# A decoder trunk on one core: the first stage in written order on all engines, with fill products on TensorE

## The chip, the core and the metric

The kernel runs on one core of a Trainium2 chip. The metric is the device time of one execution in microseconds; smaller is better. The core's engines work side by side, each through its own list of instructions in order: TensorE (PE in the profile, its weight loads PEld) multiplies, VectorE (DVE) and ScalarE (ACT) work elementwise, GpSimd (POOL) helps them, and SyncE (SP) issues the transfers. An engine that waits for a semaphore holds up everything behind it in its list.

## The reference

One layer of a decoder: a normed and modulated input goes through three token mixers, then through an MLP. What matters here is the very start and the first projections. In short:

```python
cond = silu(c)
mod = cond @ w_ada + b_ada                  # sh1, sc1, gt1, sh2, sc2, gt2
h = rms_norm(x, g_norm1) * (1.0 + sc1) + sh1
z = h @ w_in                                # q, keys, values, gates, inputs of the mixers
merged = sig(ga) * gmlp(z) @ w_up_a + sig(gb) * mlstm(z) @ w_up_b + sig(gc) * nsa(z) @ w_up_c
x = x + gt1 * (merged @ w_out)
h = rms_norm(x, g_norm2) * (1.0 + sc2) + sh2
x = x + gt2 * (square(relu(h @ w_mlp1)) @ w_mlp2)
out = rms_norm(x, g_final)
```

x is 512 x 1024, all in float32.

## The kernel before

The features are kept on the 128 partitions: h is eight blocks j of 128 features by 512 tokens. To keep float32's precision on TensorE, every operand is split into a high part in a reduced format (hi) and the rest (lo), and a product is made of hi x hi, hi x lo and lo x hi. The copy to hi is ScalarE's, the subtraction for lo is VectorE's or GpSimd's. So each block of weights goes through `w_raw` (loaded), `w_hi` and `w_lo`, the last two with two buffers each.

The first stage does this. The transfers bring the vectors, x as four blocks of 128 tokens in two halves (`x_in`), then for each feature block j the two columns of the modulation weights (`ada_raw`, 2 x 512 KB) and the first weights (`w_early`, 128 x 768). The condition goes through a silu and is spread over the partitions: `dgc` times ones gives `cond_T`, copied to `condb`. For each block of tokens ScalarE and VectorE sum the squares (L179, L181), GpSimd takes the power that makes the reciprocal root `r` (L185), both engines scale (L186, L187), TensorE transposes (L191, eight products) and both copy the transpose to `xT` (L194).

Then come eight rounds, one per feature block. `early_mod(j)` loads, splits the weights (`chunk`, L109 and L110) and makes the modulation's two sums: for j = 0 and 4 (`ADA_PE`) on TensorE, 16 products with one column each (L225, two passes each in the trace), for the others on VectorE, two sums over 1024 columns (L216) against `condb`. `early_h(j)` makes scale and offset `ab` (L228, L230), h (ScalarE, L232), `h_hi` (ScalarE, L94) and `h_lo` (VectorE, L95). TensorE then makes 18 products of the round: six hi x hi (L245) and six pairs of lo x hi and hi x lo (L249, L250), into six banks called `early`.

Behind the rounds the banks are evacuated: `early` 0 to 3 are the queries of eight heads (`q`, ScalarE L323, VectorE L324), 4 and 5 the keys (`khh` ScalarE, `kll` VectorE, L331 to L334). Meanwhile TensorE makes `zt` 0 and 1 (L120, L121, then L284), which VectorE turns into windows (`win`, L362, eight steps, and `win_r`, L369), the products of the small weights (`sm`, L421 to L426, four banks: two come free with q, two with kll), the compression of the windows (`hid`, `kcmp`, `vcmp`) and then `ztok`.

What sets the order: nothing is placed by hand but TensorE's list within the first stage, which stands in `with tc.manual_schedule(engines={PE})`. Everything else is put in order by a scheduler that simulates the engines while the program is built. So the instructions of other engines within the stage, and all that follows, may move when the stage is written otherwise.

Of the kernel before, what the change touches and what calls it, by code (L numbers as in the profile page):

```python
# [36 lines left out]
ADA_PE = (0, 4)  # L37
# [23 lines left out]
def trunk_kernel(ctx: ExitStack, tc: tile.TileContext, x, vecs, rows, late_rows, ada1, w_ada,  # L61
# [68 lines left out]
    def tsl(tb):  # L130
        return slice(tb * P, (tb + 1) * P)
# [4 lines left out]
    xt = []  # L136
# [22 lines left out]
    dgc = temp(first, "dgc", "ada", 6, width=D)  # L159
# [13 lines left out]
    for tb in range(NT):  # L173
        ss1 = small.tile([P, 2], F32, name="ss1", bufs=4)
        for hf in range(2):
            xi = xt[tb][hf]
            junk = temp(first, "junk", "ht", 3)
# [4 lines left out]
        r1 = small.tile([P, 1], F32, name="r1", bufs=4)  # L182
# [15 lines left out]
    accs_, ws_early = {}, {}

    def early_mod(j):  # L200


        raws = []
        for q in range(2):
            raw = temp(first, "ada_raw", "ada", 6, width=D)
# [4 lines left out]
        ws_early[j] = chunk(w_early[j], 768)  # L210
        if j in ADA_PE:
            accs_[j] = [(raws[k // 4][:, (k % 4) * 256:(k % 4) * 256 + 256], cond[:, k:k + 1]) for k in range(KD)]
            return
        accs_[j] = small.tile([P, 2], F32, name="ada_s2")
        for q in range(2):
            V.scalar_tensor_tensor(raws[q], raws[q], 1.0, condb, op0=ALU.mult, op1=ALU.mult,  # L216
                                   accum_out=accs_[j][:, q:q + 1])

    def early_h(j):
# [11 lines left out]
        h, hi, lo = temp(first, "h_tmp", "ht", 3), page("h", "h_hi", F32R), page("h", "h_lo", F32R)  # L231
# [1136 lines left out]
```

## Time and profile before

| | |
|---|---|
| median of 3 runs | 976.35 us (974.14 to 977.8) |
| the profiled execution | 972.84 us, its span in the trace 971.0 us |
| TensorE busy | 934.9 us, 96% of the span |
| VectorE, ScalarE, GpSimd busy | 606.3, 406.9, 168.1 us |
| mean granted clock of TensorE | 0.979 |

All times below are counted in us from the start of the span. The granted clock is 1.00 at 2.4 GHz and 0.50 at 1.2 GHz. A row of a timeline gives start, duration, engine, line, operation, what is written and read, how often, and in brackets how long the engine had been idle ahead of it and what released it. The chain of waits is followed back from the last instruction of the program to what released each step.

### The profile page before, as it was taken

The page shows a single profiled execution, that of the slowest core. Times are in us where ns is not written, and L with a number is a line of the kernel's source. Part 1 is how long each engine was busy: PE and PEld are TensorE (multiplying, and loading weights), DVE is VectorE, ACT ScalarE, POOL GpSimd, SP SyncE. Part 2 cuts the span into 40 slices and gives each one's busy share as a digit, 9 for nine tenths or more (in the row PEclk, how much of TensorE's full clock was granted, in tenths as well). Part 3 has the DMA queues.
Part 4 walks back from the last instruction along what each step waited for, and adds up shares of the span by engine and source line. Part 5 has one row for each costly group of instructions (what it writes and reads, how often), then busy time and mean ns, then how long its engine had stood idle before and what let it go on. Part 6 is the DMA issues. An engine that isn't in the chain of part 4 may idle for free.

```text
span 971.0 us, 12508 instructions
## 1 busy us (share of the span) xinstructions
PE 934.9 (96%) x4718; PEld 787.2 (81%) x4718; DVE 606.3 (62%) x1167; ACT 406.9 (42%) x786; POOL 168.1 (17%) x118
## 2 busy tenths in 40 slices
PE   5999998998999999999999998999999999999997
PEld 4789987797876888888988887988888888888886
DVE  7648588777389656656688889766424254442435
ACT  5465465665463444444333344544321223432221
POOL 3044342332344123113300003000000000000001
PEclk8899999998999999999999999999999999999999
DMA  9633210110231223222478872363233323223222
GB/s 338 231 124 100 67 44 23 44 45 22 65 109 65 67 94 99 69 86 87 160 239 257 301 246 88 91 191 121 93 103 89 106 87 106 90 88 107 87 87 87
DMA packets 34268, 111.71 MB, mean 115 GB/s; under 512 B 3936, under 2 KB 4128, under 8 KB 34208
## 3 DMA queue, kind: packets, MB, share of 16 engines
q1 hardware_dynamic: 34208, 110.91, 34.7%
q8 instruction: 37, 0.61, 0.3%
q14 instruction: 23, 0.19, 0.1%
HBM read 108.80 MB, written 2.10 MB: 114 GB/s over the span
## 4 chain that ended last, share of the span: by engine, by line
PE 84%; DVE 11%; ACT 2%; issue 1%; DMA 1%; SPq 0%; POOL 0%; POOLq 0%; ACTq 0%
PE tok L1096 7%; PE tok L1095 7%; PE tok L1097 7%; PE m L116 6%; PE m L115 6%; PE m L114 6%; PE zt L120 5%; PE zt L121 5%; PE zt L284 5%; PE ztok L896 5%; PE pv L557 2%; PE up L120 2%; PE up L121 2%; PE up L849 2%; PE pT L532 2%; PE zt L880 2%
## 5 line engine op out<-in xcount | busy, mean ns | idle before, releaser
L109 ACT CAST w_hi<-w_raw 128x1024 fp32r<-128x1024 f32 (+2 forms) x137 | 141.6, 1033 | 255.8 <-PE tok L1096 97.4
L110 DVE TENSOR_TENSOR w_lo<-w_raw,w_hi 128x1024 fp32r<-128x1024 f32 (+1 forms) x92 | 115.1, 1252 | 175.9 <-ACT w_hi L109 169.7
L110 POOL TENSOR_TENSOR w_lo<-w_raw,w_hi 128x1024 fp32r<-128x1024 f32 (+2 forms) x45 | 110.3, 2452 | 246.8 <-ACT w_hi L109 137.6
L120 PE MATMUL zt<-h_hi,w_hi 128*128 128x512 f32 x272 | 107.8, 396 | 0.0
L121 PE MATMUL zt<-h_lo,w_hi 128*128 128x512 f32 x272 | 107.3, 395 | 0.0
L116 PE MATMUL m<-h_hi,w_lo 128*128 128x512 f32 (+1 forms) x272 | 103.9, 382 | 0.0
L114 PE MATMUL m<-h_hi,w_hi 128*128 128x512 f32 (+1 forms) x272 | 103.8, 382 | 0.0
L115 PE MATMUL m<-h_lo,w_hi 128*128 128x512 f32 (+1 forms) x272 | 103.6, 381 | 0.0
L1096 PE MATMUL tok<-w_hi,f_lo 128*128 128x512 f32 (+1 forms) x232 | 88.6, 382 | 0.0
L1095 PE MATMUL tok<-w_hi,f_hi 128*128 128x512 f32 (+1 forms) x232 | 88.6, 382 | 0.0
L1097 PE MATMUL tok<-w_lo,f_hi 128*128 128x512 f32 (+1 forms) x232 | 84.3, 382 | 0.0
L284 PE MATMUL zt<-h_hi,w_lo 128*128 128x512 f32 x272 | 70.0, 393 | 0.0
L120 PEld LDWEIGHTS zt<-h_hi,w_hi 128*128 128x128 f32 x272 | 51.4, 189 | 10.9 <-ACT num_lo L778 0.4
L115 PEld LDWEIGHTS m<-h_lo,w_hi 128*128 128x128 f32 x272 | 51.1, 188 | 11.0
L121 PEld LDWEIGHTS zt<-h_lo,w_hi 128*128 128x128 f32 x272 | 51.5, 189 | 10.4
L114 PEld LDWEIGHTS m<-h_hi,w_hi 128*128 128x128 f32 x272 | 51.2, 188 | 10.5
L116 PEld LDWEIGHTS m<-h_hi,w_lo 128*128 128x128 f32 x272 | 51.1, 188 | 10.5
L284 PEld LDWEIGHTS zt<-h_hi,w_lo 128*128 128x128 f32 x272 | 50.8, 188 | 10.5
L1237 POOL TENSOR_TENSOR o_g<-x,gfin 128x512 f32<-128x512 f32 x1 | 1.3, 1293 | 310.9 <-DVE x L1141 310.9
L1095 PEld LDWEIGHTS tok<-w_hi,f_hi 128*128 128x128 f32 x232 | 43.6, 188 | 8.5
L1097 PEld LDWEIGHTS tok<-w_lo,f_hi 128*128 128x128 f32 x232 | 43.6, 188 | 8.5
L1096 PEld LDWEIGHTS tok<-w_hi,f_lo 128*128 128x128 f32 x232 | 43.6, 188 | 8.4
(388 smaller groups left out, 2000.9 us busy)
## 6 DMA issues: line engine op xcount, KB each, us to landing
w_raw<-in_w_m SPq DMA_DIRECT2D x64, 512.0 KB, 3.5
w_raw<-in_w_zt SPq DMA_DIRECT2D x38, 512.0 KB, 3.4
ada_raw<-in_w_ada SPq DMA_DIRECT2D x24, 512.0 KB, 4.9
ada_raw<-in_ada SPq DMA_DIRECT2D x14, 512.0 KB, 7.0
w_raw<-in_w_tok SPq DMA_DIRECT2D x12, 512.0 KB, 3.4
w_raw<-in_w_up SPq DMA_DIRECT2D x12, 512.0 KB, 3.5
w_raw<-in_w_out SPq DMA_DIRECT2D x8, 512.0 KB, 4.8
w_raw<-in_w_ada SPq DMA_DIRECT2D x8, 512.0 KB, 3.9
```

The lines of the kernel that those rows point to most:

```text
L109: V.tensor_copy(hi, raw) if dve_hi else A.copy(hi, raw)
L110: (G if pool_lo else V).tensor_tensor(lo, raw, f(hi), op=ALU.subtract)
L114: T.matmul(ps, ah, bh, start=first, stop=False)
L115: T.matmul(ps, ah, bl, start=False, stop=False)
L116: T.matmul(ps, al, bh, start=False, stop=last)
L120: T.matmul(ps, ah, bh, start=first, stop=False)
L121: T.matmul(ps, ah, bl, start=False, stop=False)
L284: T.matmul(ps, wl[:, tsl(k)], hh[k], start=False, stop=k == KD - 1)
L896: T.matmul(o, a_[k][:, tsl(tb)], w_[:, kk * 256:(kk + 1) * 256], start=k == 0 and tb % 2 == 0 and a_ is hh and w_ is wh, stop=k == KD - 1 ...
L1095: T.matmul(p_, ah_, wh, start=k == 0, stop=False)
L1096: T.matmul(p_, al_, wh, start=False, stop=False)
L1097: T.matmul(p_, ah_, wl, start=False, stop=k == 2 * n - 1)
```

## The change

It rewrites the first stage and leaves the arithmetic as it is.

- The stage stands in a manual order for TensorE, ScalarE, VectorE and GpSimd, not for TensorE alone: on these engines the order is that of the code. The transfers' order is still the scheduler's.
- The work on x is cut into four functions (`x_rms`, `x_scale`, `x_turn`, `x_copy`), called for different blocks of tokens in turn, so that the copy of a transpose comes a block after its scaling.
- `idle(n)` puts n products of ones by ones, 128 x 128, into a bank that nothing reads: 9, 4, 5, 3, 2 and 6 of them.
- Loads are written two rounds ahead (`early_load`), with seven buffers for `ada_raw` instead of six; the sums (`early_sums`), scale and offset (`early_mod`) and h with the split of the weights (`early_h`) are called for round j + 1 between the two halves of round j's products.
- Scratch for the squares and for h comes from other pages (tag "mr").

```diff
-    for hf in range(2):
-        cp = bank("T", "cond_T")
-        T.matmul(cp, ones, dgc[:, hf * 512:(hf + 1) * 512], start=True, stop=True)
-        A.copy(condb[:, hf * 512:(hf + 1) * 512], cp)
...
+    def idle(n):
+
+        for _ in range(n):
+            T.matmul(warm[:, 0:P], ones, ones, start=True, stop=True)
...
     def early_h(j):
-        tp = accs_.pop(j)
...
+
+        wh = stream.tile([P, D], F32R, name="w_hi", tag="hi")[:, :768]
+        wl = stream.tile([P, D], F32R, name="w_lo", tag="lo")[:, :768]
+        A.copy(wh, raw_early[j])
+        ab = abs_[j]
+        h, hi, lo = page("mr", "h_tmp"), page("h", "h_hi", F32R), page("h", "h_lo", F32R)
         A.activation(h, xT[j // 4][:, j % 4, :], AF.Identity, scale=ab[:, 0:1], bias=ab[:, 1:2])
         split(hi, lo, h)
+        V.tensor_tensor(wl, raw_early[j], f(wh), op=ALU.subtract)
+        ws_early[j] = wh, wl
...
-    with tc.manual_schedule(engines={mybir.EngineType.PE}):
+    raw_early, abs_, sums_ = {}, {}, {}
+    E_ = mybir.EngineType
+    with tc.manual_schedule(engines={E_.PE, E_.Activation, E_.DVE, E_.Pool}):
+        early_load(0)
+        early_load(1)
+        warm = bank("acc", "warm")
+        idle(9)
+        cps = [bank("T", "cond_T") for _ in range(2)]
+        for hf in range(2):
+            T.matmul(cps[hf], ones, dgc[:, hf * 512:(hf + 1) * 512], start=True, stop=True)
+        idle(4)
+        x_rms(0)
+        x_rms(1)
+        x_scale(0)
+        A.copy(condb[:, 0:512], cps[0])
+        x_turn(0)
+        idle(5)
+        x_rms(2)
+        x_scale(1)
+        x_copy(0)
+        x_turn(1)
+        idle(3)
+        x_rms(3)
+        x_scale(2)
+        x_copy(1)
+        A.copy(condb[:, 512:D], cps[1])
+        x_turn(2)
+        idle(2)
+        x_scale(3)
+        x_copy(2)
+        x_turn(3)
+        x_copy(3)
+        early_sums(0)
         early_mod(0)
+        idle(6)
         early_h(0)
+        early = [bank(t, "early") for t in ("mm", "mm", "S", "S", "acc", "acc")]
         for j in range(KD):
-            wh, wl = ws_early.pop(j)
-            if j + 1 < KD:
-                early_mod(j + 1)
+            wh, wl = ws_early[j]
+            if j + 2 < KD:
+                early_load(j + 2)
             for i in range(6):
                 T.matmul(early[i], wh[:, tsl(i)], hh[j], start=j == 0, stop=False)
             if j + 1 < KD:
+                if j + 1 not in sums_:
+                    early_sums(j + 1)
+                if j + 1 in ADA_PE and j + 2 < KD:
+                    early_sums(j + 2)
+                early_mod(j + 1)
                 early_h(j + 1)
             for i in range(6):
                 T.matmul(early[i], wh[:, tsl(i)], hl[j], start=False, stop=False)
                 T.matmul(early[i], wl[:, tsl(i)], hh[j], start=False, stop=j == KD - 1)
```

How the lists of the engines differ is shown at three places. The first is VectorE from the last copies of transposes on. The list before, in which `ada_s` are the sums of a round, `ab` its scale and offset, and `w_lo` the split of the weights:

```order
L194 COPY xT_128<-x_T 128x4x128
L110 TENSOR_TENSOR w_lo<-w_raw,w_hi 128x768
L216 SCALAR_TENSOR_TENSOR ada_raw,ada_s_318<-ada_raw,condb 128x1024 x2
L228 TENSOR_SCALAR ab<-ada_T,bsc_120,vec 128x1
L230 TENSOR_SCALAR ab<-ada_T,vec 128x1
L228 TENSOR_SCALAR ab<-ada_s_278,bsc_120,vec 128x1
L230 TENSOR_SCALAR ab<-ada_s_278,vec 128x1
L216 SCALAR_TENSOR_TENSOR ada_raw,ada_s_358<-ada_raw,condb 128x1024
L228 TENSOR_SCALAR ab<-ada_s_318,bsc_120,vec 128x1
L230 TENSOR_SCALAR ab<-ada_s_318,vec 128x1
L230 TENSOR_SCALAR ab<-ada_s_358,vec 128x1
L95 TENSOR_TENSOR h_lo<-h_tmp,h_hi 128x512
```

Before, the sums of rounds 1 to 3 (`ada_s_278`, `_318`, `_358`) stand ahead of the first `h_lo` or right behind it. The list of the changed kernel at the same place:

```order
L201 COPY xT_122<-x_T 128x4x128 x2
L242 TENSOR_SCALAR ab<-ada_T,bsc_120,vec 128x1
L244 TENSOR_SCALAR ab<-ada_T,vec 128x1
L95 TENSOR_TENSOR h_lo<-h_tmp,h_hi 128x512
L255 TENSOR_TENSOR w_lo<-w_raw,w_hi 128x768
L235 SCALAR_TENSOR_TENSOR ada_raw,ada_s_316<-ada_raw,condb 128x1024 x2
L242 TENSOR_SCALAR ab<-ada_s_316,bsc_120,vec 128x1
L244 TENSOR_SCALAR ab<-ada_s_316,vec 128x1
L95 TENSOR_TENSOR h_lo<-h_tmp,h_hi 128x512
L255 TENSOR_TENSOR w_lo<-w_raw,w_hi 128x768
L235 SCALAR_TENSOR_TENSOR ada_raw,ada_s_356<-ada_raw,condb 128x1024 x2
```

Now each round stands by itself: sums, `ab`, `h_lo`, `w_lo`, and only then the sums of the next round.

The second place is ScalarE at the end of the rounds. There `w_hi` of 768 columns is a round's, `w_hi` of 1024 columns is that of `zt`, and `q` the evacuation of the queries. Before:

```order
L109 CAST w_hi<-w_raw 128x1024
L368 CAST phi_r<-w_raw 128x16x64
L323 ACTIVATE q_0_604<-early 64x512
L323 ACTIVATE q_1_605<-early 64x512
L323 ACTIVATE q_2_606<-early 64x512
L109 CAST w_hi<-w_raw 128x1024
L323 ACTIVATE q_3_607<-early 64x512
L323 ACTIVATE q_4_612<-early 64x512
```

The evacuation of q 0 to 2 stands ahead of the weights of zt(1), the second `w_hi` of 1024 columns. In the changed kernel:

```order
L250 CAST w_hi<-w_raw 128x768
L109 CAST w_hi<-w_raw 128x1024
L253 ACTIVATE h_tmp<-xT_123,ab 128x512
L94 CAST h_hi<-h_tmp 128x512
L109 CAST w_hi<-w_raw 128x1024
L385 ACTIVATE q_0_634<-early 64x512
L430 CAST phi_r<-w_raw 128x16x64 x2
L385 ACTIVATE q_1_635<-early 64x512
L385 ACTIVATE q_2_636<-early 64x512
L385 ACTIVATE q_3_637<-early 64x512
L385 ACTIVATE q_4_642<-early 64x512
L109 CAST w_hi<-w_raw 128x864
```

The weights of zt(0) have moved ahead of the last round's h (and on TensorE fourteen of zt(0)'s products ahead of the last round's), and the weights of zt(1) and both phi stand ahead of or between the first q.

The third place is VectorE behind the rounds, where `win` is a window's step, `win_r` its split, and `kll` the evacuation of a key bank. In the changed kernel:

```order
L386 SCALAR_TENSOR_TENSOR q_0_634<-early,q_0_634 64x512
L386 SCALAR_TENSOR_TENSOR q_1_635<-early,q_1_635 64x512
L424 TENSOR_TENSOR win<-zt,vec 64x8x31 x5
L386 SCALAR_TENSOR_TENSOR q_2_636<-early,q_2_636 64x512
L424 TENSOR_TENSOR win<-zt,vec 64x8x31 x3
L386 SCALAR_TENSOR_TENSOR q_3_637<-early,q_3_637 64x512
L386 SCALAR_TENSOR_TENSOR q_4_642<-early,q_4_642 64x512
L424 TENSOR_TENSOR win<-zt,vec 64x8x31 x8
L431 TENSOR_TENSOR win_r<-win,win_r 128x16x64
L386 SCALAR_TENSOR_TENSOR q_5_643<-early,q_5_643 64x512
L386 SCALAR_TENSOR_TENSOR q_6_644<-early,q_6_644 64x512
L431 TENSOR_TENSOR win_r<-win,win_r 128x16x64
```

Before, seven q stood in a row ahead of the first window, and the first two kll ahead of and among the steps of the second; now both windows stand among the q, and all kll behind them.

## Rows read from the trace of the kernel before

**Rows 1.** Timeline of TensorE in stage one: start, us, operation, idle before.
```profile
5.04 3.78 PE L169 MATMUL cond_T<-dgc,ones 128*128 128x512 f32 x4 [5.04 <-DVE dgc L161]
...
13.88 1.71 PE L225 MATMUL ada_T<-cond,ada_raw 128*128 128x1 f32 x8
15.45 4.65 PE L191 MATMUL x_T<-ident,x_in 128*128 128x128 f32 x24
19.93 1.84 PE L225 MATMUL ada_T<-cond,ada_raw 128*128 128x1 f32 x16
26.52 2.93 PE L245 MATMUL early<-h_hi,w_hi 128*128 128x512 f32 x6 [4.74 <-ACT h_hi L94]
```

**Rows 2.** Timeline of VectorE in stage one.
```profile
13.88 0.48 DVE L187 TENSOR_SCALAR x_in<-x_in,r 128x512 f32<-128x512 f32 x1
...
21.71 1.22 DVE L216 SCALAR_TENSOR_TENSOR ada_raw<-ada_raw,condb 128x1024 f32<-128x1024 f32 x1
...
24.00 0.27 DVE L228 TENSOR_SCALAR ab<-ada_T,bsc,vec 128x1 f32<-128x1 f32 x1
```

**Rows 3.** The chain of waits up to 112 us: start, us, what.
```profile
32.27 1.36 PE early L245 x6
...
76.20 1.22 DVE win_r L369
...
86.14 0.71 DVE kll L333
```

**Rows 4.** Timeline of TensorE from round 3 to vcmp.
```profile
41.62 3.63 PE L225 MATMUL ada_T<-cond,ada_raw 128*128 128x1 f32 x32
45.11 0.48 PE L249 MATMUL early<-h_lo,w_hi 128*128 128x512 f32 x1
...
49.14 1.91 PE L245 MATMUL early<-h_hi,w_hi 128*128 128x512 f32 x6
...
69.47 1.98 PE L284 MATMUL zt<-h_hi,w_lo 128*128 128x512 f32 x8
...
94.99 0.33 PE L896 MATMUL ztok<-w_hi,h_hi 128*128 128x256 f32 x1
...
103.60 0.66 PE L399 MATMUL vcmp<-p,c_rep 64*128 64x64 f32 x4 [1.33 <-DVE c_rep L397]
```

**Rows 5.** Timeline of VectorE in round 3, whose h it waits for.
```profile
31.27 0.69 DVE L95 TENSOR_TENSOR h_lo<-h_tmp,h_hi 128x512 fp32r<-128x512 f32 x1 [1.54 <-ACT h_hi L94]
...
33.02 0.95 DVE L110 TENSOR_TENSOR w_lo<-w_raw,w_hi 128x768 fp32r<-128x768 f32 x1
```

**Rows 6.** Stretches: us, busy of PE, PEld, DVE, ACT, POOL, granted clock, DMA share, GB/s.
```profile
9.00:12.00 3.00, 0.63 (x6) 0.66 (x6) 2.46 (x10) 2.28 (x7) 1.42 (x3) 1.00 1.00 345
...
15.40:19.00 3.60, 3.60 (x18) 3.60 (x19) 3.21 (x5) 0.63 (x2) 0.00 (x0) 0.50 1.03 418
19.30:21.80 2.50, 2.48 (x24) 2.39 (x22) 2.50 (x5) 1.64 (x3) 0.00 (x0) 1.00 1.04 380
...
46.60:49.60 3.00, 3.00 (x9) 2.35 (x8) 3.00 (x10) 2.49 (x4) 0.22 (x2) 0.50 0.00 0
...
104.80:107.40 2.60, 2.60 (x14) 2.60 (x14) 0.00 (x0) 0.00 (x0) 1.40 (x1) 0.50 0.07 13
```

**Rows 7.** Timeline of ScalarE behind the rounds.
```profile
63.99 0.59 ACT L323 ACTIVATE q<-early 64x512 fp32r<-64x512 f32 x1
...
71.05 0.92 ACT L109 CAST w_hi<-w_raw 128x864 fp32r<-128x864 f32 x1
```

**Rows 8.** Timeline of VectorE behind the rounds.
```profile
71.84 3.00 DVE L362 TENSOR_TENSOR win<-zt,vec 64x248 f32<-64x248 f32 x8
...
95.18 1.95 DVE L95 TENSOR_TENSOR v<-v,v 128x256 fp32r<-128x256 f32 x1
...
98.35 0.49 DVE L95 TENSOR_TENSOR v<-v,v 128x256 fp32r<-128x256 f32 x1
```

**Rows 9.** Timeline of GpSimd at the same time.
```profile
94.45 2.40 POOL L110 TENSOR_TENSOR w_lo<-w_raw,w_hi 128x1024 fp32r<-128x1024 f32 x1 [1.60 <-ACT v L94]
```

More of the change, by code (lines that the diff above doesn't have):

```diff
@@ L157, in trunk_kernel @@
     V.tensor_scalar(cond, cth, 0.5, None, op0=ALU.mult)
-    dgc = temp(first, "dgc", "ada", 6, width=D)
+    dgc = temp(first, "dgc", "ada", 7, width=D)
     for k in range(KD):
@@ L164, in trunk_kernel, with x_rms @@
     V.tensor_scalar(bsc1, vec[:, V_SC1:V_SC1 + 8], 1.0, None, op0=ALU.add)
-    for hf in range(2):
-        cp = bank("T", "cond_T")
-        T.matmul(cp, ones, dgc[:, hf * 512:(hf + 1) * 512], start=True, stop=True)
-        A.copy(condb[:, hf * 512:(hf + 1) * 512], cp)
     xT = [first.tile([P, 4, S], F32, name=f"xT{hf}") for hf in range(2)]
-    for tb in range(NT):
+    r1s = {}
+    def x_rms(tb):
         ss1 = small.tile([P, 2], F32, name="ss1", bufs=4)
@@ L176, in trunk_kernel @@
             xi = xt[tb][hf]
-            junk = temp(first, "junk", "ht", 3)
+            junk = page("mr", "junk")
             if hf == 0:
@@ L181, in trunk_kernel @@
                 V.scalar_tensor_tensor(junk, xi, 1.0, xi, op0=ALU.mult, op1=ALU.mult, accum_out=ss1[:, 1:2])
-        r1 = small.tile([P, 1], F32, name="r1", bufs=4)
+        r1 = r1s[tb] = small.tile([P, 1], F32, name="r1", bufs=4)
         V.tensor_tensor(r1, ss1[:, 0:1], ss1[:, 1:2], op=ALU.add)
@@ L185, in trunk_kernel, with x_scale, x_turn, x_copy @@
         G.tensor_tensor(r1, r1, mhalf[:, 0:1], op=ALU.pow)
-        A.activation(xt[tb][0], xt[tb][0], AF.Copy, scale=r1)
-        V.tensor_scalar(xt[tb][1], xt[tb][1], r1, None, op0=ALU.mult)
+    def x_scale(tb):
+        A.activation(xt[tb][0], xt[tb][0], AF.Copy, scale=r1s[tb])
+        V.tensor_scalar(xt[tb][1], xt[tb][1], r1s[tb], None, op0=ALU.mult)
+    x_ps = {}
+    def x_turn(tb):
+        x_ps[tb] = [bank(("mm", "S", "acc")[(2 * tb + hf) % 3], "x_T") for hf in range(2)]
         for hf in range(2):
-            tp = bank(("mm", "S", "acc")[(2 * tb + hf) % 3], "x_T")
             for q in range(4):
-                T.transpose(tp[:, tsl(q)], xt[tb][hf][:, tsl(q)], ident)
+                T.transpose(x_ps[tb][hf][:, tsl(q)], xt[tb][hf][:, tsl(q)], ident)
+    def x_copy(tb):
+        for hf in range(2):
             dst = xT[hf][:, :, tsl(tb)]
-            src = tp.rearrange("p (q t) -> p q t", q=4)
+            src = x_ps[tb][hf].rearrange("p (q t) -> p q t", q=4)
             A.copy(dst, src) if hf else V.tensor_copy(dst, src)
+    def idle(n):
+        for _ in range(n):
+            T.matmul(warm[:, 0:P], ones, ones, start=True, stop=True)
     hh, hl = [], []
-    early = [bank(t, "early") for t in ("mm", "mm", "S", "S", "acc", "acc")]
     accs_, ws_early = {}, {}
-    def early_mod(j):
+    def early_load(j):
         raws = []
         for q in range(2):
-            raw = temp(first, "ada_raw", "ada", 6, width=D)
+            raw = temp(first, "ada_raw", "ada", 7, width=D)
             for c0 in range(0, D, 512 if j == 0 else D):
@@ L209, in early_mod, with early_sums @@
             raws.append(raw)
-        ws_early[j] = chunk(w_early[j], 768)
+        accs_[j] = raws
+        raw_early[j] = load(w_early[j], 768)
+    def early_sums(j):
+        raws = accs_[j]
         if j in ADA_PE:
[L212 to L219, printed above, removed]
-        tp = accs_.pop(j)
-        if j in ADA_PE:
-            ts_, tp = tp, bank("T", "ada_T")
-            for i, (a, c_) in enumerate(ts_):
-                for u in range(2):
-                    T.matmul(tp[:, u:u + 1], a[:, u * P:(u + 1) * P], c_, start=i == 0 and u == 0,
-                             stop=i == len(ts_) - 1 and u == 1)
-        ab = small.tile([P, 2], F32, name="ab")
+            tp = bank("T", "ada_T")
+            for k in range(KD):
+                for u in range(2):
+                    T.matmul(tp[:, u:u + 1], raws[k // 4][:, (k % 4) * 256 + u * P:(k % 4) * 256 + (u + 1) * P],
+                             cond[:, k:k + 1], start=k == 0 and u == 0, stop=k == KD - 1 and u == 1)
+        else:
+            tp = small.tile([P, 2], F32, name="ada_s2")
+            for q in range(2):
+                V.scalar_tensor_tensor(raws[q], raws[q], 1.0, condb, op0=ALU.mult, op1=ALU.mult,
+                                       accum_out=tp[:, q:q + 1])
+        sums_[j] = tp
+    def early_mod(j):
+        tp = sums_[j]
+        ab = abs_[j] = small.tile([P, 2], F32, name="ab")
         V.tensor_scalar(ab[:, 0:1], tp[:, 1:2], bsc1[:, j:j + 1], vec[:, V_G1 + j:V_G1 + j + 1], op0=ALU.add,
@@ L230, in early_h @@
         V.tensor_scalar(ab[:, 1:2], tp[:, 0:1], vec[:, V_SH1 + j:V_SH1 + j + 1], None, op0=ALU.add)
-        h, hi, lo = temp(first, "h_tmp", "ht", 3), page("h", "h_hi", F32R), page("h", "h_lo", F32R)
+    def early_h(j):
+        wh = stream.tile([P, D], F32R, name="w_hi", tag="hi")[:, :768]
[3 more added lines that the diff above has]
+        h, hi, lo = page("mr", "h_tmp"), page("h", "h_hi", F32R), page("h", "h_lo", F32R)
         A.activation(h, xT[j // 4][:, j % 4, :], AF.Identity, scale=ab[:, 0:1], bias=ab[:, 1:2])
         split(hi, lo, h)
+        V.tensor_tensor(wl, raw_early[j], f(wh), op=ALU.subtract)
+        ws_early[j] = wh, wl
         hh.append(hi)
         hl.append(lo)
-    with tc.manual_schedule(engines={mybir.EngineType.PE}):
+    raw_early, abs_, sums_ = {}, {}, {}
[6 more added lines that the diff above has]
+        cps = [bank("T", "cond_T") for _ in range(2)]
+        for hf in range(2):
+            T.matmul(cps[hf], ones, dgc[:, hf * 512:(hf + 1) * 512], start=True, stop=True)
[22 more added lines that the diff above has]
+        early_sums(0)
         early_mod(0)
+        idle(6)
         early_h(0)
+        early = [bank(t, "early") for t in ("mm", "mm", "S", "S", "acc", "acc")]
         for j in range(KD):
-            wh, wl = ws_early.pop(j)
-            if j + 1 < KD:
-                early_mod(j + 1)
+            wh, wl = ws_early[j]
+            if j + 2 < KD:
+                early_load(j + 2)
             for i in range(6):
```

## The prediction

> **What bounds the kernel now.** I read the page first, then TensorE's timeline from the start, the stretches with the granted clock, VectorE's timeline beside it, and last the chain of waits up to 112 us. TensorE is busy for 96% of the span, so a change of its work elsewhere would count in full; but the instruction order of all engines is the same again from about 112 us on, so only the first 112 us can differ, and what is won or lost there is carried to the end. In that stretch three things are to be seen. First, TensorE starts its real work late: the first product of block 0 starts at 26.52 [rows 1]. The products for the modulation of block 0 had ended at 19.93 + 1.84 = 21.77 [rows 1], but VectorE took their result only at 24.00, behind two sums for block 2 that stand ahead of it, the first at 21.71 [rows 2]. Second, up to about 58 us TensorE is the bound: 18 products of a block at 1.36 / 6 = 0.227 each, 4.09 in all [rows 3]. Third, from 64 to 87 us the chain runs through VectorE and ScalarE (the evacuation of q, the windows, k) and ends with a kll on VectorE at 86.14 [rows 3]; TensorE's products just keep up with them. So VectorE is the second bound here, and a change that hands it work later is paid for.
>
> I measure against a mark M: TensorE has done all products of the eight blocks and the first sixteen of zt(0). Before, M is 69.47 [rows 4].
>
> **Stage one: fills and order.** VectorE scales the last block of x at 13.88 + 0.48 = 14.4 even before [rows 2]; now one copy of a transpose stands ahead of that, so 14.4 to 15.0. The eight transposes behind it take 24 per 4.65, so 1.5, at the half clock [rows 1], and I bound them below by half of that: done at 15.2 to 16.5. Now the 16 modulation products of block 0 (32 passes in the trace) follow at once: 3.6 at the full clock [rows 4], or 4 x 1.71 = 6.8 at half [rows 1]. Then ab, about 0.4, and the 1.54 from the last ab to the end of h_hi [rows 5], with nothing ahead of them on VectorE any more. So h_hi(0) is ready between 20.7 and 25.2 instead of 26.5. I take 22.7, nearer to the full clock, since the fills keep TensorE at work from the start on: a gain of **3.8** (1.3 to 5.8).
>
> A fill, ones by ones 128x128, isn't in the trace. The nearest row is cond_T, four passes of 512 columns in 3.78 [rows 1], so by columns 2 x 0.24 = 0.47 at half clock; below it is bounded by two modulation passes, 0.22. The first nine, 4.2, thus all but fit into the 5.04 that TensorE waited for cond_T's operand; cond_T's result is first read by the sums of block 1, so what they run over is hidden. The fills between the transposes lie in waits for the scaled x. The last six cost 1.3 to 2.8 beside the 1.95 of ab and h; that can hold up block 0's products by 0.9, but not the chain of VectorE below, which starts at h_hi(0). If the cover is gone, it is 0.9.
>
> Where the clock stands at the modulation products decides most of that range. TensorE ran transposes alone from 15.45 to 19.9, and its granted clock went from 0.50 to 1.00 by 19.30 [rows 1, 6]: transposes were enough to raise it to 2.4 GHz from 1.2. The Trainium skill (TensorE: Matmul & The Clock Gate, Part 4: PE-mode transpose) says that the full clock does not engage for transposes as it does for matmuls; this trace does not agree. By the page the slow end, 25.2, would be the likelier one and the sum below 2.5 us higher.
>
> **The eight blocks.** This is where the gain goes. Before, VectorE made the sums of blocks 1 to 3 ahead, while TensorE still waited for block 0. Now its order is strict: h_lo(j), w_lo(j), two sums of j+1, ab(j+1), then a wait for ScalarE's h and h_hi, then h_lo(j+1). One round is 0.69 + 0.95 [rows 5] + 2.29 for the two sums (21.71 to 24.00, [rows 2]) + 0.4 + 1.54 [rows 5], less 0.1 where neighbours overlap: 5.8, against 4.09 for TensorE's block. So TensorE waits some 1.7 in each of the first three rounds, and block 3 starts 17.4 after h_hi(0). Block 3 holds the modulation products of block 4, 3.5 (41.62 to 45.11 [rows 4]), so it takes 7.6; block 4's round brings VectorE the sums of block 5 in that time. Blocks 4 and 5 are then TensorE's, 4.09 each; block 6 starts at +16.0, when its h_hi is ready, and ends at +20.1. Now zt(0) stands ahead of block 7 on TensorE; its weights' copy waits for block 6's buffer, so TensorE waits 1.0, then does 34 products, 7.7: M at +28.8. If the clock falls behind the modulation products as before (12 products in 49.14 - 45.11 = 4.03 for 2.72 [rows 4], clock 0.50 [rows 6]), +30.3. So 46.2 to 47.7 from h_hi(0) to M, where it was 69.47 - 26.5 = 43.0: a loss of 3.2 to 4.7, I take **3.8**. The half clock that the waits may bring in the first three rounds costs no more, since it only fills the waits.
>
> **From M to ztok.** Before, 94.99 - 69.47 = 25.5 [rows 4]. There VectorE began with q before M, since ScalarE evacuated q0 at 63.99 [rows 7]. Now ScalarE copies the weights of zt(1) first, which waits for block 7's buffer, so q0 starts at M + 1.0, then come both phi copies, and VectorE's q1 follows at M + 4.2. From there by the new orders: window 0 and q2, q3, q4 to 9.9 (eight windows take 3.00 [rows 8], a q 0.65), window 1 to 12.9, win_r 1.22 [rows 3] to 14.1, two q, win_r, q, two kll and the small steps between them to 19.9. The copy of the small weights, 0.92 [rows 7], stands behind q4 on ScalarE and ends at M + 9.6, though zt(1) is done at 7.3: a wait of 2.3. The third bank of sm waits for the second kll until 19.9, where TensorE is ready at 17.3: another 2.6. The rest is 10.1 of products. So ztok starts at M + 30.0: a loss of 4.5. If VectorE's chain runs without gaps it is 2.1 shorter, loss 2.4; if the second wait brings the half clock, 1.5 longer, loss 6.0. I take **5.0**.
>
> **vcmp.** Before, TensorE waited 1.33 ahead of it [rows 4] and then ran at 0.50 [rows 6], some 1.5 more. Now c_hid(1) no longer stands behind a table load, but vcmp comes only 32 products (3.8) behind ztok's start, with VectorE's copies of v in front of it. Between all of it gone, -2.8, and a wait 1.7 longer, I take **0**.
>
> **The DMA order** is nearly unchanged: seven buffers for ada instead of six let one more load go early. No round waits for a load, since each is issued a round or more ahead. The buffers of raw weights come free with w_lo, later than before, still in time.
>
> **Sum:** -3.8 + 3.8 + 5.0 + 0 = +5.0. The profiled execution took 972.84 (span 971.0), 3.5 below the median of the runs, 976.35; so 977.8 against that execution, and 981.4 as a median. The ends of the terms give -3.0 and +11.1, so 973.4 to 987.5.
>
> **Rivals.**
> (a) The stage comes out even or better, not slower: the fills hold 2.4 GHz through stage one (h_hi(0) at 20.7, -5.8), the blocks cost 3.2, VectorE's chain behind M has few gaps (+3.5) and half of vcmp's loss goes (-1.4): -0.5, 975.9. For it speaks that cond_T's four passes were followed by the full clock, 1.00 from 9 to 12 us [rows 6]; against it, that all ends must be met at once. It decides from h_hi(0) before 21.5 together with less than 4 us lost behind M.
> (b) VectorE and GpSimd get in each other's way. A v step of VectorE took 1.95 at 95.18, where the same took 0.49 at 98.35 [rows 8], while GpSimd's w_lo ran from 94.45 for 2.40 [rows 9]. In the new order win_r of window 0 falls at M + 12.9, and GpSimd's w_lo of the second small chunk at 12.6 to 14.7: 1.8 more; and v stands ahead of vcmp: 1.6 more. +8.4, 984.8. The Trainium skill (SBUF — State Buffer, Who interferes with whom) has this as a rule: a VectorE instruction with two SBUF inputs and a GpSimd one that reads SBUF block each other whole; the trace agrees.
> (c) The fills don't do what they are for: the modulation products run at the half clock and h_hi(0) comes at 25.2: +7.5, 983.9.
>
> **Chances.** Forecast 0.55, (a) 0.22, (b) 0.14, (c) 0.09. A measurement of this kernel tells about 0.5%, 4.9 us, from no change. The forecast (+2 to +8) is half beyond that; (a) is nearly all within; (b) and (c) nearly all beyond: slower 0.48, same 0.46, faster 0.06. The range leaves out the best of (a) and the worst of (b): 975 to 988.
>
> **What would show it.** h_hi(0) between 20.7 and 25.2; rounds of 5.8 with TensorE waiting 1.5 to 1.8 for h_hi in the first three; a wait of 1 ahead of zt(0); sm waiting for the small weights and for kll by 2 to 3 each; ztok some 5 us later than 94.99. I am wrong if the rounds are 4.1, if M comes before 66, or if sm waits for nothing.

## The result: slower, and the loss lies behind the blocks

The changed kernel takes 983.48 us (median of 7 runs, 979.11 to 985.28), the kernel before, beside it on the same chip, 974.14 (7 runs, 971.46 to 977.8). The ratio is 1.0086, with a 95% interval of 1.0058 to 1.0114: slower by 0.9%, beyond the 0.5% that a measurement of this kernel can tell. The predicted 981.4 is 2.1 below it, and the range of 975 to 988 holds it. The profiled execution took 981.23, its span is 979.5, so 8.5 more than the 971.0 of before. TensorE was busy for 944.1 us instead of 934.9. The page's first part for the changed kernel (busy us, share, instructions):

```profile
span 979.5 us, 12612 instructions
PE 944.1 (96%) x4776; PEld 793.9 (81%) x4776; DVE 607.7 (62%) x1167; ACT 406.7 (42%) x786; POOL 170.1 (17%) x118
```

TensorE's timeline of the changed kernel up to the first S product (start, us, operation, count, idle before):

```profile
1.11 3.64 PE L206 MATMUL warm<-ones 128*128 128x128 f32 x18 [1.11 <-DVE ones L149]
...
15.31 4.68 PE L230 MATMUL ada_T<-cond,ada_raw 128*128 128x1 f32 x32
...
22.41 2.58 PE L302 MATMUL early<-h_hi,w_hi 128*128 128x512 f32 x6
...
33.61 1.66 PE L302 MATMUL early<-h_hi,w_hi 128*128 128x512 f32 x6 [1.41 <-ACT h_hi L94]
...
39.41 1.65 PE L302 MATMUL early<-h_hi,w_hi 128*128 128x512 f32 x6 [1.38 <-ACT h_hi L94]
...
62.18 0.50 PE L120 MATMUL zt<-h_hi,w_hi 128*128 128x512 f32 x1 [0.91 <-ACT w_hi L109]
...
65.50 1.52 PE L302 MATMUL early<-h_hi,w_hi 128*128 128x512 f32 x6
...
70.03 1.98 PE L346 MATMUL zt<-h_hi,w_lo 128*128 128x512 f32 x8
...
78.25 0.40 PE L483 MATMUL sm<-w_hi,h_hi 128*128 128x288 f32 x1 [0.81 <-ACT w_hi L109]
...
90.70 0.58 PE L483 MATMUL sm<-w_hi,h_hi 128*128 128x288 f32 x1 [3.46 <-DVE kll L395]
...
95.29 0.69 PE L454 MATMUL kcmp<-c_hid,p 64*128 64x64 f32 x2
...
104.44 0.38 PE L958 MATMUL ztok<-w_hi,h_hi 128*128 128x256 f32 x1 [0.79 <-ACT gate L495]
...
120.66 0.30 PE L564 MATMUL S<-khh,q 128*128 128x128 f32 x1 [0.17 <-DVE cbias L520]
```

In the kernel before, the same S product stood here:

```profile
112.25 0.30 PE L502 MATMUL S<-khh,q 128*128 128x128 f32 x1 [0.17 <-DVE cbias L458]
```

It comes 8.41 later, so the whole loss is made by then. Divided at the prediction's marks (h_hi(0) ready, M, the first product of ztok, the first S product), in us:

| | h_hi(0) | h_hi(0) to M | M to ztok | ztok to S |
|---|---|---|---|---|
| before [rows 1, 4] | 26.5 | 43.0 | 25.5 | 17.3 |
| after | 21.9 | 48.1 | 34.4 | 16.2 |
| difference | -4.6 | +5.1 | +8.9 | -1.0 |
| predicted | -3.8 | +3.8 | +5.0 | 0 |

Stage one gains what was predicted, and the eight blocks lose it again, as predicted. Between M and ztok nearly twice as much is lost as predicted. There VectorE's timeline reads:

```profile
69.35 0.68 DVE L386 SCALAR_TENSOR_TENSOR q<-early,q 64x512 fp32r<-64x512 f32 x1 [3.33 <-ACT q L385]
...
81.87 2.53 DVE L431 TENSOR_TENSOR win_r<-win,win_r 128x1024 fp32r<-128x1024 f32 x1
...
85.87 1.23 DVE L431 TENSOR_TENSOR win_r<-win,win_r 128x1024 fp32r<-128x1024 f32 x1
...
89.86 0.69 DVE L395 TENSOR_TENSOR kll<-early,khh 64x512 fp32r<-64x512 f32 x1
...
91.89 0.21 DVE L450 SCALAR_TENSOR_TENSOR c_t<-c_t,c_hid 64x64 f32<-64x64 f32 x1
...
104.52 1.62 DVE L450 SCALAR_TENSOR_TENSOR c_t<-c_t,c_hid 64x64 f32<-64x64 f32 x1
...
107.70 2.35 DVE L711 TENSOR_TENSOR lf<-lf,mg 128x16 f32<-128x16 f32 x1
```

The first q starts 0.7 ahead of M and the second kll ends at 90.55; the third bank of `sm` waits 3.46 for it.

### The profile page after: what moved, and what is told of

Its sections match the earlier page's. It is cut to its first block, busy times and chain, and to the rows that moved or that the text cites. A ratio compares the mean times of both kernels' runs of the same rounds, so it can differ in the third digit from the quotient of the medians.

```text
span 979.5 us, 12612 instructions
## 1 busy us (share of the span) xinstructions
PE 944.1 (96%) x4776; PEld 793.9 (81%) x4776; DVE 607.7 (62%) x1167; ACT 406.7 (42%) x786; POOL 170.1 (17%) x118
## 4 chain that ended last, share of the span: by engine, by line
PE 81%; DVE 13%; ACT 2%; issue 2%; DMA 2%; POOL 0%; POOLq 0%; SPq 0%; ACTq 0%; DVEq 0%
PE tok L1157 7%; PE tok L1158 6%; PE tok L1159 6%; PE m L114 6%; PE m L115 6%; PE m L116 6%; PE zt L120 5%; PE zt L121 5%; PE zt L346 5%; PE ztok L958 4%; PE pv L619 2%; PE up L120 2%; PE up L121 2%; PE up L911 2%; PE pT L594 2%
## 5 line engine op out<-in xcount | busy, mean ns | idle before, releaser
L109 ACT CAST w_hi<-w_raw 128x1024 fp32r<-128x1024 f32 (+1 forms) x129 | 134.8, 1045 | 254.1 <-PE tok L1158 97.5
L110 DVE TENSOR_TENSOR w_lo<-w_raw,w_hi 128x1024 fp32r<-128x1024 f32 x84 | 107.4, 1278 | 169.2 <-ACT w_hi L109 162.2
```

## The experiments

My theory was the prediction's: the strict rounds of VectorE cost the eight blocks what the stage gains, and the new order of evacuation behind M costs the rest. Each part was undone or done alone. The kernels keep the changed stage unless the diff says otherwise; all ratios are to the kernel before.

**The strict order on three engines.** Here only TensorE's list is by hand, as before the change; the new code, its fills and its order on TensorE stay.

```diff
-    with tc.manual_schedule(engines={E_.PE, E_.Activation, E_.DVE, E_.Pool}):
+    with tc.manual_schedule(engines={E_.PE}):
```

> The changed code with the manual order set back to TensorE alone, as in the kernel before: fills, the cut x functions and the seven buffers stay, but ScalarE, VectorE and GpSimd are ordered by the scheduler, which again puts sums of rounds 1 and 2 ahead of the first ab and the weights of zt(0) behind block 7. Theory (the loss comes from the strict order on VectorE and all that follows from its slow rounds): h_hi(0) at 22 to 25, since sums stand ahead of ab again, TensorE's rounds 4.1, M at 66 to 68, q 5 ahead of M, ztok 25.5 to 27 behind it, 968 to 972. Rival (something else in the new code, the buffers, the pages or the fills, costs it): 976 or more.

Measured: 970.94, ratio 0.9969 (0.9950 to 0.9989), some 12 below the changed kernel. TensorE's timeline of two rounds and of ztok:

```profile
28.52 1.52 PE L302 MATMUL early<-h_hi,w_hi 128*128 128x512 f32 x6
...
32.60 1.52 PE L302 MATMUL early<-h_hi,w_hi 128*128 128x512 f32 x6
...
93.32 0.33 PE L958 MATMUL ztok<-w_hi,h_hi 128*128 128x256 f32 x1
```

VectorE makes sums ahead again, and the modulation products end 0.8 later than in the changed kernel, at 20.81; so `ab` of block 0 starts at 21.59 instead of 20.03, and h_hi(0) is ready at 24.05. Rounds last 4.08; M is at 67.56 and ztok 25.76 behind it. The strict lists of the other engines thus carry the loss, and they also carry 2.1 of the stage's gain of 4.6. The other 2.5 stay with the rest of the new code.

**The sums one step earlier.** One statement puts the sums of the next block into VectorE's wait for ScalarE's h.

```diff
         A.activation(h, xT[j // 4][:, j % 4, :], AF.Identity, ...)
+        if j + 1 < KD and j + 1 not in ADA_PE and j + 1 not in sums_:
+            early_sums(j + 1)
         split(hi, lo, h)
```

> The changed kernel with one move: VectorE makes the two sums of round j+1 while it waits for h of round j, ahead of h_lo(j) instead of behind w_lo(j). Theory (VectorE's strict order sets the rounds of 5.8 us): a round becomes 0.69 + 0.95 + 0.4 + 2.3 = 4.3 us, TensorE waits under 0.4 in each of the first rounds, M comes 4 to 5 us earlier (65 to 66.5 instead of 70.0), and since the evacuation's order behind M also comes out nearer to that of before, the whole time falls by 5 to 10, to 973 to 978. Rival one (ScalarE's copies and h, or a load, set the round, VectorE only follows): rounds stay at 5.8 and the time at 983. Rival two (the whole loss is made behind M): M moves to 66, but the first ztok stays near 104, and the time at 982 to 984.

> The same kernel as e1_sums_ahead, again, beside e12 on the same chip, to tell what the fills are worth. e1 and e8 stood at 0.9926 and 0.9958, from different sessions. Theory one (fills worth nothing; in e8's profile the clock fell once more behind the modulation products of block 4, as it also does in some kernels with fills): this and e12 within 0.15% of each other. Theory two (fills are worth some 2 us): 0.2 to 0.4% apart, e12 the slower.

Measured: 967.05, ratio 0.9926 (0.9900 to 0.9952); the same kernel again, 969.81, 0.9958 (0.9936 to 0.9980). VectorE's timeline of the first run:

```profile
22.09 0.69 DVE L95 TENSOR_TENSOR h_lo<-h_tmp,h_hi 128x512 fp32r<-128x512 f32 x1
...
26.15 0.69 DVE L95 TENSOR_TENSOR h_lo<-h_tmp,h_hi 128x512 fp32r<-128x512 f32 x1
...
30.22 0.69 DVE L95 TENSOR_TENSOR h_lo<-h_tmp,h_hi 128x512 fp32r<-128x512 f32 x1
```

Rounds of 4.07, and none of these rows ends in a wait for h_hi. In the changed kernel the same rows come 5.81 apart, each behind such a wait:

```profile
21.97 0.69 DVE L95 TENSOR_TENSOR h_lo<-h_tmp,h_hi 128x512 fp32r<-128x512 f32 x1 [1.53 <-ACT h_hi L94]
...
27.78 0.69 DVE L95 TENSOR_TENSOR h_lo<-h_tmp,h_hi 128x512 fp32r<-128x512 f32 x1 [1.53 <-ACT h_hi L94]
```

So the two sums fill 1.53 of VectorE's time that lay empty. M and ztok in the first run:

```profile
63.31 1.98 PE L348 MATMUL zt<-h_hi,w_lo 128*128 128x512 f32 x8
...
90.03 0.33 PE L960 MATMUL ztok<-w_hi,h_hi 128*128 128x256 f32 x1
```

The direction was expected, the size was not: rounds of 4.3, M at 65 to 66.5 and 973 to 978 in all. From h_hi(0) to M it is 41.9 (42.9 in the second run) instead of 48.1, and M to ztok also falls, from 34.4 to 26.7, though nothing behind M was edited. The scheduler now puts zt(0) behind block 7 by itself, as it does in the kernel with the strict list on TensorE alone; both have rounds of 4.07 or 4.08, in which TensorE doesn't wait for block 7's h. That made the place of zt(0) a second suspect.

**The evacuation against the place of zt(0).** First the order of ScalarE and VectorE behind the blocks, written out as before the change; zt(0) stays ahead of block 7:

```diff
-    for h in range(8):
-        evac_q(h)
...
+    with tc.manual_schedule(engines={E_.Activation, E_.DVE}):
+        ps0 = zt(ZT_NKC, True, "T")
+        for h in range(3):
+            evac_q(h)
+        ps1 = zt(ZT_NVC, True, "T")
+        for h in range(3, 5):
+            evac_q(h)
+        phi(0)
...
```

> The changed kernel, its first stage untouched, with one move behind it: ScalarE and VectorE take the queries, the windows, the keys and the copies of the weights in the order of the kernel before (q0 to q2 ahead of the weights of zt(1), both phi behind q4 and q6, seven q ahead of window 0, the first kll ahead of win_r). Theory (the order of the evacuation costs the 8.9 us between M and ztok): M stays at 69 to 70, ztok starts 25.5 to 27.5 behind it instead of 34.4, no half clock from 90 to 96, the whole time falls by 7 to 9, to 974.5 to 977. Rival (the loss behind M is contention between VectorE and GpSimd, whose steps now fall together in any order): ztok starts 30 or more behind M, and the time falls by under 4.

Measured: 975.75, ratio 1.0031 (1.0005 to 1.0057). M and ztok:

```profile
68.96 1.98 PE L346 MATMUL zt<-h_hi,w_lo 128*128 128x512 f32 x8
...
99.70 0.38 PE L1026 MATMUL ztok<-w_hi,h_hi 128*128 128x256 f32 x1
```

M to ztok is 30.7. That gives back 3.7 of the 8.9; more was expected, and the rival's 30 or more is met, though the whole time fell as the theory had it. Then the other half alone: zt(0) held behind block 7 on TensorE and ScalarE, the evacuation left to the scheduler.

```diff
...
                 T.matmul(early[i], wl[:, tsl(i)], hh[j], start=False, stop=j == KD - 1)
+        ps0 = zt(ZT_NKC, True, "T")
...
-    windows(0, zt(ZT_NKC, True, "T"), V_PEK)
+    windows(0, ps0, V_PEK)
```

> The changed kernel with one move: zt(0) is held behind block 7; the evacuation is left to the scheduler, which with that alone puts q0 to q2 ahead of the weights of zt(1), and seven q ahead of the end of window 0. Theory (the place of zt(0) is what brought the late evacuation): M 48.5 to 49.2 behind h_hi(0), the first q on VectorE 5 ahead of M, ztok 26 to 28 behind M, and 971.5 to 974, within 2 of e5, where the evacuation was ordered by hand as well. Rival (both moves are needed): ztok 30 or more behind M, 976 or more.

Measured: 971.30, ratio 0.9982 (0.9960 to 1.0003). VectorE's first q in this kernel, and then in the kernel with the evacuation of before:

```profile
63.76 0.68 DVE L387 SCALAR_TENSOR_TENSOR q<-early,q 64x512 fp32r<-64x512 f32 x1 [1.24 <-ACT q L386]
```

```profile
67.52 0.68 DVE L386 SCALAR_TENSOR_TENSOR q<-early,q 64x512 fp32r<-64x512 f32 x1 [2.56 <-ACT q L385]
```

TensorE's timeline of the kernel with zt(0) behind:

```profile
60.99 1.65 PE L312 MATMUL early<-h_hi,w_hi 128*128 128x512 f32 x6 [1.43 <-ACT h_hi L94]
...
68.86 1.98 PE L267 MATMUL zt<-h_hi,w_lo 128*128 128x512 f32 x8
...
85.96 0.37 PE L484 MATMUL sm<-w_hi,h_hi 128*128 128x288 f32 x1 [0.75 <-DVE kll L396]
...
93.95 0.33 PE L959 MATMUL ztok<-w_hi,h_hi 128*128 128x256 f32 x1
```

The rounds still wait for h_hi (1.43), but M to ztok is 25.1, below the 26 to 28 expected and as before the change, and of the waits of `sm` 0.75 is left. With block 7 ahead of zt(0) its first bank is done 5.8 us before M and its last 3.5, the first q stands at M - 5.1 and, with nothing said on it, q 0 to 2 go ahead of the weights of zt(1) again. With zt(0) ahead, even the old order of evacuation starts only at M - 1.4. Both halves together:

```diff
...
+        ps0 = zt(ZT_NKC, True, "T")
...
+    with tc.manual_schedule(engines={E_.Activation, E_.DVE}):
+        for h in range(3):
+            evac_q(h)
...
```

> As e2_evac_as_before, and besides zt(0) is held behind block 7 on TensorE and ScalarE, as in the kernel before (in the changed kernel and in e2 fourteen of its products stand ahead of block 7). e2 brought only half of what was expected behind M; theory: the other half is the place of zt(0), which lets block 7, and with it the first query, end late: q starts 1.4 before M in e2, 4.9 before M in the kernel before. Then TensorE waits 2 to 3 for the h of block 7, M comes 1 to 1.5 later than in e2 counted from h_hi(0) (49.0 to 49.6 instead of 48.1), q starts 4.5 to 5.5 before M, ztok starts 26 to 27.5 behind M instead of 30.7, and from h_hi(0) to the first product of the scores it is 92 to 93.5 instead of 93.9: 973.5 to 975.5 as a median. Rival (the evacuation is late for its own length, wherever zt(0) stands): ztok stays 30 behind M, the time rises to 977.

Measured: 971.97, ratio 0.9991 (0.9972 to 1.0011), a little below the 973.5 to 975.5 expected; M to ztok is 26.8, as expected, and that is nothing that zt(0) alone didn't bring. So the place of zt(0) is the cause of the loss from M to ztok, and the late evacuation follows from it. Why zt(0) was put ahead is not shown by a run of its own: it stands there in the kernels with rounds of 5.8 where nothing holds it, and behind block 7 in those with rounds of 4.07 or 4.08, where TensorE doesn't wait for block 7's h.

**What GpSimd adds.** Its split of the first two small chunks is replaced by zeros written ahead, so the low half of those weights is left out of the products:

```diff
...
+        if c < 2:
+            G.memset(f(wl), 0.0)
+        else:
+            G.tensor_tensor(wl, raw, f(wh), op=ALU.subtract)
```

> The changed kernel, all orders kept, but GpSimd does not compute the low part of the first two chunks of the small weights: it writes zeros there and reads nothing (this part of the product is left out). Theory (GpSimd's subtraction beside it is what made the split of window 0 take 2.53 us on VectorE where the second took 1.23): the split takes 1.2 to 1.3, everything on VectorE behind it comes 1.3 earlier, and with the wait for the third small bank 1.3 shorter the whole time falls by 1.3 to 3, to 980.5 to 982. Rival (the split took longer for another reason, or any GpSimd access is enough): it still takes 2.5 and the time stays at 983.5.

Measured: 980.24, ratio 1.0071 (1.0042 to 1.0101). VectorE's win_r of window 0 in this kernel:

```profile
82.17 1.23 DVE L431 TENSOR_TENSOR win_r<-win,win_r 128x1024 fp32r<-128x1024 f32 x1
```

In the changed kernel that row was 2.53, and GpSimd's timeline there:

```profile
81.27 2.05 POOL L110 TENSOR_TENSOR w_lo<-w_raw,w_hi 128x864 fp32r<-128x864 f32 x1 [0.89 <-ACT w_hi L109]
...
103.67 6.36 POOL L110 TENSOR_TENSOR w_lo<-w_raw,w_hi 128x1024 fp32r<-128x1024 f32 x2
```

GpSimd's step ended at 83.32, and win_r 1.08 behind it, nearly the 1.23 that it takes alone: it had got little done before. The overlap costs 1.3 on the chain to the second kll. M to ztok falls by 2.1, of which 0.8 lies behind the third bank, where the clock fell later this time. The wait of the third bank stays at 3.46, against expectation, since TensorE is ready for that bank 1.2 earlier as well. The whole time can't be told from the changed kernel's: the price is real and small. The Trainium skill (SBUF — State Buffer, Who interferes with whom) says that the two engines share a port pair that is locked exclusively; 2.53 beside GpSimd's step and 1.23 without it agree.

**What the half clock adds.** Behind the wait of 3.46 the granted clock is 0.51. Stretches of the changed kernel (us, busy of PE, PEld, DVE, ACT, POOL, granted clock, DMA share, GB/s), the second from the third bank of `sm` to kcmp:

```profile
90.00:96.30 6.30, 5.60 (x23) 5.24 (x23) 3.78 (x10) 2.56 (x6) 0.00 (x0) 0.51 0.00 0
90.70:95.30 4.60, 4.60 (x19) 4.32 (x19) 3.06 (x8) 1.65 (x4) 0.00 (x0) 0.50 0.00 0
```

In the next kernel 26 products that nothing reads fill the wait. To hold their place, the compression of window 0 stands in written order on TensorE.

```diff
+        if n == 0:
+            fp = bank("T", "fill")
+            for m in range(26):
+                T.matmul(fp[:, 0:128], phis[n][:, m % 16].rearrange("p s c -> p (s c)"),
+                         wins[n][:, m % 16].rearrange("p s c -> p (s c)"), start=True, stop=True)
...
-    compress(0)
+    with tc.manual_schedule(engines={E_.PE}):
+        compress(0)
```

> The changed kernel with 26 more products that nothing reads on TensorE, right where it waits 3.46 us for the keys ahead of the third bank of the small weights; orders up to there are unchanged, behind it some steps of the compression come out earlier, so the place to read is the third and fourth bank themselves: 18 products, 4.59 us (90.70 to 95.29) at 0.50 in the changed kernel. Theory (the wait let the clock fall, and that costs half of these 4.6): granted clock 1.00 there and 2.4 to 2.6 us. Rival (the clock falls there for another reason, or the fills run late and push the bank): 4.4 or more. The whole time: 980 to 982 by theory, 983 or more by the rival.

Its TensorE timeline and the stretch of the two banks:

```profile
86.16 3.07 PE L444 MATMUL fill<-win_r,phi_r 128*128 128x128 f32 x26
...
89.70 0.40 PE L488 MATMUL sm<-w_hi,h_hi 128*128 128x288 f32 x1 [0.46 <-DVE kll L395]
```

```profile
89.70:92.20 2.50, 2.50 (x18) 2.42 (x18) 2.38 (x6) 1.56 (x4) 2.50 (x2) 1.00 0.00 0
```

The clock stays at 1.00 and the two banks take 2.5 instead of 4.60. The half clock therefore costs 2.1 there. The whole, 980.56, ratio 1.0077 (1.0050 to 1.0105), lies where it was expected but can't be told from the changed kernel's 1.0086 (1.0058 to 1.0114): the scheduler chose other orders behind this place, so ztok and S can't be compared one for one.

**What the fills bring.** They are taken out of the changed kernel, and twice out of the kernel with the sums ahead, the second time beside that kernel on the same chip.

```diff
-        for _ in range(n):
+        for _ in range(0):
             T.matmul(warm[:, 0:P], ones, ones, start=True, stop=True)
```

> The changed kernel without its 29 fill products; orders behind the rounds come out a little different, so the place to read is the first h_hi (ready at 21.94 with fills, 26.5 in the kernel before) and the granted clock ahead of it. Theory one (the gain of 4.5 us comes from the order on VectorE, which takes block 0's modulation at once): h_hi(0) comes at 22 to 23.5, later only by what the transposes and modulation products lose at 0.50. Theory two (the fills hold the clock and bring most of the gain): h_hi(0) at 24 to 25.5. The whole time follows it by the same amount, if the waits behind it stay: 983.5 to 987.

> e1_sums_ahead without the 29 fill products. e4 had h_hi(0) at 21.2 without fills, as early as with them, so theory: fills are worth nothing, h_hi(0) at 20.7 to 21.9, rounds 4.1, 966 to 968. Rival (with short rounds the clock at the start of block 0 counts, since TensorE now has no wait to absorb it): block 0 takes 1 to 2 longer, 968 to 969.5.

> The same kernel as e8_sums_no_fills, again, beside e11. Theory one (fills worth nothing): 967 to 968, and the granted clock behind the modulation products of block 4 at 1.00 in this profile. Theory two: 969, 0.2 to 0.4% above e11, and the clock falls there again.

Measured without fills: 981.02, ratio 1.0069 (1.0043 to 1.0094), below the 983.5 to 987 expected; with the sums ahead 968.96, 0.9958 (0.9939 to 0.9977), and 971.61, 0.9976 (0.9956 to 0.9996), the first in its rival's range, the second above what either theory gave it. TensorE's timeline of the changed kernel without fills, where block 0's products start at 21.23:

```profile
14.94 4.29 PE L230 MATMUL ada_T<-cond,ada_raw 128*128 128x1 f32 x32
21.23 2.93 PE L302 MATMUL early<-h_hi,w_hi 128*128 128x512 f32 x6 [1.99 <-ACT h_hi L94]
```

h_hi(0) is ready at 21.2, earlier than either theory had it and within the 20.6 to 22.4 of the kernels with fills and the strict lists. So the gain of stage one comes from the rewritten stage without the fills. On one chip the kernel with the sums ahead took 969.81 with fills and 971.61 without; by the ratios, 0.9926 and 0.9958 with and 0.9958 and 0.9976 without, the fills are ahead as well, but the intervals overlap: whether they bring up to 0.3% or nothing stays open.

**A better version.** The sums ahead, the evacuation by hand with the second kll in the middle of window 1, and the four copies of kll behind all else:

```diff
...
+            early_sums(j + 1)
...
+        kll_a(1, 1)
+        for br in range(2):
+            for g in range(2):
+                kll_b(br, g)
```

> The order of e1_sums_ahead, and behind it by hand: the four copies of kll to the other half (the first took 2.17 beside GpSimd, ahead of window 1) go behind all four subtractions and both splits, and the second kll goes into the middle of window 1. Theory (VectorE's chain behind M ends the wait of TensorE for the third and fourth small bank, 1.44 + 0.81 in e1): both waits go, ztok starts 24.5 to 25.5 behind M instead of 26.7, 965 to 966 against 967.05. Rival (the copies only move their 2 us to another wait, of the second window or of the compression): 966.5 to 968.

Measured: 965.77, ratio 0.9921 (0.9893 to 0.9949): faster than before by 0.8%, the lowest of all, though its interval does not part it from the sums ahead alone. M to ztok is 24.1, and `sm` waits for nothing:

```profile
63.65 1.98 PE L348 MATMUL zt<-h_hi,w_lo 128*128 128x512 f32 x8
...
87.76 0.33 PE L1027 MATMUL ztok<-w_hi,h_hi 128*128 128x256 f32 x1
```

## Why the prediction was right, point by point

- **Stage one** (-3.8 predicted, -4.6): right. The modulation products took 4.68, between the bounds of 3.6 and 6.8, and ended at 19.99 instead of 21.77 [rows 1]; `ab` followed at 20.03 instead of 2.2 later [rows 2]. Together that is 4.0 of the 4.6. The reason given for a time near the full clock, the fills, was not: without them h_hi(0) came no later. Rival (c), h_hi(0) at 25.2, fell with it.
- **The eight blocks** (+3.8, measured +5.1): the mechanism and the round were right to the tenth. Rounds came 5.81 apart, block 3 started 17.47 behind h_hi(0), and the wait ahead of zt(0) was 0.91 (1.0 predicted). TensorE waited in two of the first three rounds, 1.41 and 1.38, a little under 1.5 to 1.8; in the first, block 0's products filled the time: the last fills held them up by 0.5, and then they ran at the half clock (2.58 for the six that take 1.52 at the full one). The sums ahead took the loss away (41.9 and 42.9, against 43.0 before). The term was 1.3 too small and 0.4 above its range of 3.2 to 4.7. Of the price of the half clock behind the modulation products, 1.5 in that range, only 0.6 had been taken; it measured 1.7 (12 products from 44.40 to 48.82, for 2.72). The clock was 0.50 there, as it had been before [rows 6]:

```profile
45.60:48.40 2.80, 2.80 (x8) 2.13 (x8) 1.86 (x4) 0.85 (x2) 0.00 (x0) 0.50 0.05 16
```

- **From M to ztok** (+5.0, measured +8.9, and so above its range of 2.4 to 6.0): this is the mis-sized term, and ztok came 9.45 later than before, not some 5. The chain that was to decide it did: the second kll ended at M + 20.5 where 19.9 was predicted, although its parts were off both ways (ScalarE started q 0 at 68.74, 2.3 ahead of M + 1.0; win_r lasted 1.3 longer). The failed step is "the rest is 10.1 of products": from the third bank to ztok it was 13.74. Of the 3.6 missing, 2.1 is the half clock on the two banks, which stood in the range as "1.5 longer" and of which 0.5 was taken; 0.79 is a wait ahead of ztok that no step named; the rest, 0.7, is partly the half clock on the products up to 96.3. The waits for the small weights were over-sized, 2.3 against 0.81.
- **The cause of that term** was half right. The prediction laid it on ScalarE, which copies the weights of zt(1) before it evacuates q, and priced zt(0) ahead of block 7 at its own wait of 1.0. The runs show that zt(0) ahead of block 7 is what makes the evacuation late; given back its place, 25.1 came back without another word on the evacuation.
- **vcmp** (0, measured -1.0): within its bounds. It waited 1.72 for c_rep instead of 1.33 [rows 4], but no half clock followed: the granted clock was 1.00 from 110.25 to 113.00.
- **Rival (a)** fell: h_hi(0) did not come before 21.5, and more than 4 us were lost behind M. **Rival (b)** was right in its first half (win_r 2.53, 1.3 more, 1.8 predicted). In its second half it was wrong in the victims: two v steps took only 0.74 together beside GpSimd's w_lo, and two small steps on the way to c_rep took 1.62 and 2.35; but vcmp waited only 0.4 longer than before.

The terms missed by -0.8, +1.3, +3.9 and -1.0, in sum +3.4: the profiled execution took 981.23 where 977.8 was predicted. The median lies 2.25 above that execution, not 3.5 as the prediction took over from before, so it was missed by 2.1 only. That closeness is in part luck: two of the four terms left their own ranges, the other two and the step from the execution to the median were off the other way, and the range held for the sum alone.

## What to carry to other kernels

When an order is written out for an engine, look at what it waits for in each round and put the next round's independent work into that wait: two sums moved by one step took 1.7 us off VectorE's rounds here, and TensorE's block 3 started 14.3 behind h_hi(0) instead of 17.5. A scheduler can move work into a wait that looks harmless on one engine, and that move can cost more than the wait: find in the new order what has been put into each new gap, and price what it delays further on.

## What the runs showed of the hardware

The granted clock fell while TensorE was counted busy without a gap. In the changed kernel this is so in the later part of the one-column modulation products (15.31 to 19.99) and in the fills behind them:

```profile
18.30:22.20 3.90, 3.90 (x19) 3.90 (x20) 0.64 (x3) 1.70 (x3) 0.00 (x0) 0.50 1.02 402
```

And it is not fixed by the program. The kernel with the sums ahead, run twice, had either level at the same place behind the modulation products of block 4; first one execution, then the other:

```profile
41.00:43.00 2.00, 2.00 (x11) 1.65 (x10) 0.46 (x3) 1.44 (x2) 0.00 (x0) 1.00 0.00 0
```

```profile
41.00:43.00 2.00, 2.00 (x6) 1.56 (x6) 1.06 (x2) 0.87 (x2) 0.00 (x0) 0.50 0.00 0
```

M, counted from h_hi(0), came at 41.9 and 42.9; in the same kernel without fills, also run twice, at 45.8 (where the 0.50 lasted longer) and 43.1. A term of a few us that rests on the clock of one execution is no surer than that.

Transposes also held the full clock. Without fills, TensorE did nothing but transposes from 8.8 to 14.9 us. Of the first sixteen nine took 0.42 each; in the stretch behind them one took 0.27 to 0.28, and the granted clock was:

```profile
12.00:15.00 3.00, 2.08 (x18) 1.85 (x18) 2.43 (x6) 2.44 (x5) 0.72 (x1) 1.00 1.04 420
```

The rule that the prediction weighed, from the Trainium skill (TensorE: Matmul & The Clock Gate, Part 4: PE-mode transpose), does not hold for these float32 transposes: in [rows 6] the clock rose among them, and in this stretch it stayed.

Small VectorE steps beside GpSimd's w_lo stretch as far as large ones: c_t of 64x64 took 1.62, where the same line took 0.21 at 91.89, and lf of 128x16 took 2.35. GpSimd's row from 103.67 on holds two steps: one of 2.39, to 106.06, and one of 4.03, to 110.03. The first VectorE step ended at 106.14 and the second at 110.05, each with the GpSimd step beside it. The size of a step says nothing of that price. GpSimd pays too: VectorE's v steps and what stands among them ran from 106.06 to 107.7 at their usual pace, and the GpSimd step that started there took 4.03, where one took 2.40 in [rows 9].
